# A later norm, a solve in equal portions and ScalarE copies in the chunked scan of a hybrid encoder

## The chip, the cores and the metric

The program runs on one core of a Trainium2 chip. A core has a matrix engine (TensorE, PE in the profile), a vector engine (VectorE, DVE), a scalar engine (ScalarE, ACT), a general engine (GpSimd, POOL) and a queue processor that here only issues transfers (SyncE, SP). Each engine executes its own instructions strictly in order; they wait for each other by semaphores. The metric is the device time of one execution in microseconds, the median of several runs.

## The reference

Two token sequences (256 and 1024 tokens, 1024 channels, 16 heads of 64) go through two layers with the same weights. Layer 0 mixes tokens with a bidirectional RWKV-7 scan, layer 1 with neighbourhood attention, and each is followed by a squared-ReLU MLP. The part that matters here is the scan, run once forward and once backward per head, and the norm behind it:

```python
def step(S, inp):
    r_t, w_t, k_t, v_t, a_t, b_t = inp
    sa = jnp.einsum('bhvk,bhk->bhv', S, a_t)
    S = S * w_t[:, :, None, :] + sa[..., None] * b_t[:, :, None, :] + v_t[..., None] * k_t[:, :, None, :]
    return S, jnp.einsum('bhvk,bhk->bhv', S, r_t)
...
mu = jnp.mean(y, axis=-1, keepdims=True)
var = jnp.mean(jnp.square(y - mu), axis=-1, keepdims=True)
y = ((y - mu) * lax.rsqrt(var + GN_EPS)).reshape(B, T, C) * lnx_g + lnx_b
y = y + (bonus * vf).reshape(B, T, C)
out = (y.astype(h.dtype) * g) @ w_o
```

Here `y` is the sum of both directions, `g` a gate per token and channel, `bonus` a number per token and head.

## The kernel before

The kernel has these stages: dense projections of layer 0 (`l0_proj`), a preparation of the scan's operands that shares the engines with the last projections, the scan (`scan`), then layer 0's output projection and MLP (`channel_layer`), attention, and layer 1's. All dense products are in fp32, split in a high and a low part.

**The scan** works on chunks of 64 tokens. A *job* is 16 chunks of a pair of heads; there are ten jobs, and each step of a job takes one chunk forward and one backward. The written order of the scan is a list of pairs (time, piece of work): `at(t, f)` enters `f` at time `16 j + t` for job `j`, and the list is sorted by time (`scan_until`). That order is kept on PE, DVE, ACT and POOL; SP's order is chosen by the framework. One unit of this time is called a *slot* here: step `i` of a job stands at `16 j + i`. A time outside 0 to 16 falls into the slots of a neighbouring job, so that the stages of several jobs are interleaved:

- *Early products* (L817 to L844; from `T0` = -41 on, eight groups two slots apart): SP loads `eab`, PE multiplies into `aps`, DVE multiplies by a triangular mask into `za` (L837), SP stores `za` to `dd` in DRAM (L840).
- *Rows for the solve* (`mload`, L848, at `T1 = T0 + 17.8`): SP reads `dd` back in another layout into `mt` and `mraw` (L859), POOL copies one half of `mt` transposed (`mtr`, L864, four copies), and clears `q`.
- *The solve* (`rank1`, L870): 31 rows of a triangular system of 32 x 32 blocks, each row two DVE operations, `tmp` (L880) and `q` (L882), and single ones at both ends (L876). From `T2 = T0 + 20.8` on the rows are handed out by an accumulated cost, mostly two rows at one time, 0.67 slots apart, until `T3` = -10.2. `mt`, `mraw` and `q` have one buffer each.
- *Results of the solve* (`qst` L888, `qld` L905): POOL transposes `q` into `qt` (L894), SP stores both to `qd` and loads them back into `Q` and `qx` (tiles `qq`, `qx`; L911, L912).
- *Merges* (L921 to L943; from -5 on): PE multiplies `za` by `qx` into `yps`, ACT copies; PE multiplies into `qps`, ACT copies into `Q`. All these PE results, `aps` and `zps` too, share two PSUM banks.
- *Chunk products* (L955 to L980): four slots ahead of its step, PE computes a chunk pair's products in `kps` (one buffer), ACT copies one part (`ll`, L973), DVE masks the other (`zz`, L968).
- *The step* (`scan_step`): PE, ACT copy `up` (L1043), PE, ACT copy `u` (L1062), PE, two ACT operations for the state `S` (L1077), and the output `y` (L1082, L1085); in the second half of a job DVE adds both directions (L1089).
- *The norm* (`scan_post`): a job's outputs are normed in two halves. Half 0 starts at `t0` = 12.9 of the job, half 1 at 20.9 (in the last job 16.9). Its pieces: `p0` bonus times `vv` on DVE (+0.2), `lnx(1)` the bias added to `bv` on POOL (+0.7), `p1` mean and `p2` centring on DVE (+0.6, +0.95), `p2b` square on ACT (+1.45), `p2c` sum on DVE, `p3` the inverse root on DVE and ACT, `p4` scaling on DVE (+2.5), `lnx(0)` the gain on POOL (L1128, +3.1), `tr` 16 transposing matmuls that add `bv` (`zps`, L1169, +5.4), `p5` a copy on ACT (`zt`, L1173, +5.7) and eight transfers that POOL issues (`z_d`, L1178).

The first jobs' early work is different. Job 0's stands in the preparation's own list (`begin`, L463, maps its times onto that list), and job 1's and a little of job 2's stand in a ramp ahead of the first step. Behind the scan, `gated` multiplies each normed tile by the gate, `t = t * ps` (L1323), and splits it for the output projection.

Of the kernel before, what the change touches and what calls it, by code (L numbers as in the profile page):

```python
# [13 lines left out]
P = 128  # L14
# [15 lines left out]
V_QG, V_KG = 136, 137  # L30
NVEC = 138
# [18 lines left out]
class Trunk:  # L50
# [50 lines left out]
    def l0_proj(self):  # L101
# [361 lines left out]
        def begin():  # L463
            bctx.close()
            self.scan_begin()

            hi, c = -6.0, ((-42.0, tb), (-19.0, tb + 6.0), (-6.0, tb + 17.0))
            for x in self.todo:
                if x[3] < 3 and x[0] <= hi:
                    (x0, t0), (x1, t1) = c[:2] if x[0] < -19.0 else c[1:]  # L470
# [279 lines left out]
    def scan(self):  # L750
# [11 lines left out]
        self.lnx = rp.tile([P, 2, 8, 64], F32, name="lnx")  # L762
        nc.sync.dma_start(self.lnx.rearrange("p a m v -> p (a m v)"), self.a["lnx"])
# [36 lines left out]
    def scan_job(self, j):  # L800
# [8 lines left out]
        b4 = lambda t, n: t.unsqueeze(1).to_broadcast([P, 4, n])  # L809
# [5 lines left out]
        T0 = (-39.0, -39.0, -41.0)[j] if j < 3 else -41.0  # L815
# [4 lines left out]
        for n, (d, g) in enumerate(order):  # L820
# [7 lines left out]
            def prod(h, d=d, g=g):  # L828
# [6 lines left out]
                else:  # L835
                    J["za", d, g] = self.nxt(self.r_za)
                    nc.vector.tensor_tensor(out=J["za", d, g], in0=J["pa"], in1=b4(self.mask[d][:, 0:64], 64), op=ALU.mult)  # L837
# [30 lines left out]
        T3, load, pace = T2, 0.0, (-10.2 - T2) / 15  # L868
        for jj in range(31, 0, -1):
# [129 lines left out]
    def scan_step(self, at, J, st, grp, k, i, new, end):  # L999
# [59 lines left out]
        def s2c():  # L1059
            A, Y, sn, U = banks()  # L1060
            R["u"] = self.sp.tile([P, 2, 64], F32, name="u", tag="u", bufs=2)
# [11 lines left out]
        def s3c():  # L1073
            A, Y, sn, U = banks()
            S = st["S"] = self.sp.tile([P, 2, 64], F32, name="S", tag="S", bufs=3)
# [27 lines left out]
    def scan_post(self, at, J, grp, left):  # L1103

        nc = self.nc
        for half in range(2):
# [16 lines left out]
            def lnx(k, st=st, runs=runs, y=y):  # L1123
                t = (y(), st["bv"].rearrange("p (x c) v -> p x c v", x=2))[k]
                for x in range(1 if runs[0][0] == runs[1][0] else 2):
                    sl = slice(0, 2) if runs[0][0] == runs[1][0] else slice(x, x + 1)
                    w = self.lnx[:, k, runs[x][0]].unsqueeze(1).unsqueeze(1).to_broadcast([P, sl.stop - sl.start, 4, 64])
                    nc.gpsimd.tensor_tensor(out=t[:, sl], in0=t[:, sl], in1=w, op=(ALU.mult, ALU.add)[k])  # L1128
# [42 lines left out]
            def p5(st=st, runs=runs):  # L1171
                zt = self.yp.tile([P, 4, 2, 64], F32, name="zt", tag="ysq", bufs=1)
# [6 lines left out]
            t0 = (12.9, 20.9 if left else 16.9)[half]  # L1179
            if left == 0 and half == 1:  # L1180
                when = (-2.0, -1.9, -0.1, 0.0, 0.1, 0.2, 0.3, 0.4, 0.5, 0.6, 0.65, 0.7, 0.9)
            else:
                when = (0.2, 0.7, 0.6, 0.95, 1.45, 1.75, 1.9, 2.05, 2.25, 2.5, 3.1, *((5.4, 5.7) if left else (4.36, 4.62)))
            for dt, f in zip(when, (p0, lambda f=lnx: f(1), p1, p2, p2b, p2c, lambda f=p3: f(0), lambda f=p3: f(1), lambda f=p3: f(2), p4,
                                    lambda f=lnx: f(0), tr, p5)):
# [122 lines left out]
    def gated(self, wk, pm, src):  # L1308

        nc, act = self.nc, self.act  # L1310
        with self.gctx, self.tc.tile_pool(name="go", bufs=1, reuse_waits="tile", side="right") as gp:
            (sh, sl, ss), (gh, gl, gs) = self.gate
            todo = [(0, k) for k in range(KT)] + [(s, k) for s in (1, 2) for k in range(KT - 1)] + [(1, KT - 1), (2, KT - 1)]
            for s, k in todo:
# [8 lines left out]
                nc.vector.tensor_tensor(out=t, in0=t, in1=ps[:, :n], op=ALU.mult)  # L1323
# [576 lines left out]
def host_layout(inputs):  # L1900
# [25 lines left out]
        np.tile(i["na_q_g"][0], 2)[:, None], np.tile(i["na_k_g"][0], 2)[:, None]], 1)  # L1926
    o["lnx"] = np.stack([np.repeat(i[nm].reshape(8, 2, 64)[:, ::o].transpose(1, 0, 2), 64, 0) for nm, o in (("rw_lnx_g", 1), ("rw_lnx_b", -1))], 1).reshape(P, 1024)
# [36 lines left out]
```

## Time and profile before

| | |
|---|---|
| median of 3 runs | 4191.82 us |
| lowest, highest | 4188.74, 4197.66 us |
| the profiled execution | 4200.27 us |
| its span, from the first to the last instruction | 4198.5 us |
| PE busy | 3843.4 us, 92% |
| DVE busy | 2497.5 us, 59% |
| ACT busy | 1519.9 us, 36% |
| POOL busy | 1294.8 us, 31% |
| first copy `up` of the scan, last one | 770.5 us, 1437.2 us |
| jobs in the scan | 10, of 16 steps |

In a line of a group, "out<-in" are the tiles written and read, then the shapes, "x" and a count; behind the first bar stand the busy microseconds and the mean nanoseconds of one, behind the second the idle time of that engine just before, and what ended it. A line of waits reads: engine, tile and line that waited, what it waited for, microseconds in total, times, the longest. A line of a timeline has start, duration, engine (an engine's name with q is its queue processor, which issues transfers), line, operation, tiles, and in brackets the idle time before it. A line of stretches has its limits and length, then for PE, PE's weight loads, DVE, ACT and POOL the busy time with the number of instructions, the granted share of PE's clock, the mean busy share of the transfer engines, and GB/s.

### The profile page before, as it was taken

The numbers are of one execution on the slowest core, as the hardware profiler recorded it, in microseconds if no ns is written. First come the engines' busy times: TensorE is split into PE (matmuls) and PEld (weight loads), VectorE is DVE, ScalarE is ACT, GpSimd is POOL, SyncE is SP. The second block draws the span as 40 slices with busy tenths as digits, with TensorE's granted clock in tenths as the row PEclk, the third lists the DMA queues.
The fourth block names the chain that finished last, engine by engine and source line by source line (L and its number), as shares of the span: only waits on it lengthen the run. The fifth ranks groups of instructions, "written<-read, shape, count | busy, mean of one in ns | idle before, by whom it ended". The sixth has DMA issues, their size and how long they took to land.

```text
span 4198.5 us, 87027 instructions
## 1 busy us (share of the span) xinstructions
PE 3843.4 (92%) x35188; PEld 3264.8 (78%) x35188; DVE 2497.5 (59%) x4851; ACT 1519.9 (36%) x3651; POOL 1294.8 (31%) x1234
## 2 busy tenths in 40 slices
PE   7887879787888799999999999989988999999999
PEld 4665669687778687888888889867767888888888
DVE  7888973566666457555555562366665755555555
ACT  6776651343444442111111132455554311111111
POOL 5440001133333434222222241244344422222222
PEclk9997889798989899999999999999999999999999
DMA  3326555766564351111111115333334111111111
GB/s 113 87 98 205 195 194 144 199 162 167 152 171 127 88 162 51 36 41 41 36 36 41 41 51 162 96 78 70 81 91 147 61 36 36 41 41 41 36 36 61
DMA packets 385794, 393.48 MB, mean 94 GB/s; under 512 B 161872, under 2 KB 306480, under 8 KB 384112
## 3 DMA queue, kind: packets, MB, share of 16 engines
q1 hardware_dynamic: 331760, 315.42, 26.5%
q10 hardware_dynamic: 46704, 61.35, 4.2%
q0 software_dynamic: 6928, 11.15, 0.9%
q8 instruction: 276, 4.52, 0.4%
q14 instruction: 126, 1.03, 0.1%
HBM read 277.80 MB, written 121.24 MB: 95 GB/s over the span
## 4 chain that ended last, share of the span: by engine, by line
PE 62%; DVE 8%; issue 3%; DMA 3%; POOL 3%; ACT 2%; SPq 1%; ACTq 0%; DVEq 0%; POOLq 0%
PE ps L96 17%; PE ps L98 17%; PE ps L97 17%; PE bx L1001 2%; PE by L1001 1%; DVE q L882 1%; PE kps L963 1%; DVE tmp L880 1%; PE op L1879 1%; PE pt L1821 1%; DVE zz L968 1%; POOL z_d L1178 1%; PE vps L512 1%; PE vps L513 1%; PE vps L514 1%
## 5 line engine op out<-in xcount | busy, mean ns | idle before, releaser
L1436 DVE TENSOR_TENSOR x<-ps,x 128x256 f32<-128x256 f32 x1488 | 813.9, 594 | 629.7 <-PE ps L98 629.3
L96 PE MATMUL ps<-ah,whi 128*128 128x512 f32 (+1 forms) x2304 | 844.7, 367 | 4.9 <-ACT whi L90 4.2
L98 PE MATMUL ps<-ah,wlo 128*128 128x512 f32 (+1 forms) x2304 | 824.8, 358 | 1.8 <-POOL wlo L91 1.8
L97 PE MATMUL ps<-al,whi 128*128 128x512 f32 (+1 forms) x2304 | 824.4, 358 | 0.0
L91 POOL TENSOR_TENSOR wlo<-raw,whi 128x1024 fp32r<-128x1024 f32 (+1 forms) x178 | 390.2, 2192 | 860.9 <-ACT whi L90 833.4
L96 PE MATMUL ps<-hh,whi 128*128 128x512 f32 (+1 forms) x1536 | 548.3, 357 | 11.6 <-DVE x L1436 11.6
L98 PE MATMUL ps<-hh,wlo 128*128 128x512 f32 (+1 forms) x1536 | 547.0, 356 | 0.0
L97 PE MATMUL ps<-hl,whi 128*128 128x512 f32 (+1 forms) x1536 | 546.5, 356 | 0.0
L96 PEld LDWEIGHTS ps<-ah,whi 128*128 128x128 f32 x2304 | 439.7, 191 | 79.6 <-issue 13.2
L98 PEld LDWEIGHTS ps<-ah,wlo 128*128 128x128 f32 x2304 | 438.8, 190 | 67.8 <-POOL wlo L91 2.5
L97 PEld LDWEIGHTS ps<-al,whi 128*128 128x128 f32 x2304 | 439.7, 191 | 60.0 <-issue 1.1
L90 ACT CAST whi<-raw 128x1024 fp32r<-128x1024 f32 (+1 forms) x206 | 200.7, 974 | 703.8 <-PE ps L97 631.5
L96 PEld LDWEIGHTS ps<-hh,whi 128*128 128x128 f32 x1536 | 292.4, 190 | 55.0 <-DVE x L1436 14.0
L1415 POOL TENSOR_TENSOR rl<-rl 128x512 f32<-128x512 f32 (+1 forms) x192 | 174.3, 908 | 500.2 <-PE ps L98 458.3
L98 PEld LDWEIGHTS ps<-hh,wlo 128*128 128x128 f32 x1536 | 292.3, 190 | 41.4
L97 PEld LDWEIGHTS ps<-hl,whi 128*128 128x128 f32 x1536 | 292.3, 190 | 41.3
L1414 ACT ACTIVATE rl<-ps 128x512 f32<-128x512 f32 (+1 forms) x192 | 100.8, 525 | 546.0 <-PE ps L98 546.0
L1417 ACT CAST hh<-rl 128x512 fp32r<-128x512 f32 (+1 forms) x192 | 105.5, 549 | 320.9 <-POOL rl L1415 320.9
L968 DVE TENSOR_TENSOR zz<-kps,cst 128x512 f32<-128x512 f32 x160 | 110.0, 688 | 178.5 <-ACT ll L973 178.3
L1418 DVE TENSOR_TENSOR hl<-rl,hh 128x512 fp32r<-128x512 f32 (+1 forms) x192 | 119.3, 621 | 151.6 <-ACT hh L1417 151.1
L963 PE MATMUL kps<-x 64*64 64x128 f32 (+1 forms) x2560 | 167.6, 327 | 43.1 <-DVE zz L968 40.2
L1814 POOL TENSOR_TENSOR s<-s,mx 128x384 f32<-128x384 f32 (+1 forms) x154 | 116.8, 769 | 213.0 <-DVE mx L1813 149.6
(314 smaller groups left out, 7958.4 us busy)
## 6 DMA issues: line engine op xcount, KB each, us to landing
x<-x_d SPq DMA_DIRECT2D x88, 512.0 KB, 4.6
raw<-in_w_down_dram SPq DMA_DIRECT2D x64, 512.0 KB, 3.5
raw<-in_w_up_dram SPq DMA_DIRECT2D x64, 512.0 KB, 3.5
eab<-x_d SPq DMA_DIRECT2D x80, 256.0 KB, 3.3
x_d<-ar ACTq DMA_DIRECT2D x32, 512.0 KB, 3.1
x_d<-bk ACTq DMA_DIRECT2D x32, 512.0 KB, 4.3
bs<-tab SPq DMA_DIRECT2D x128, 96.0 KB, 3.9
v_d<-vt ACTq DMA_DIRECT2D x80, 128.0 KB, 4.1
```

What stands on the lines that cost most here:

```text
L90: nc.scalar.copy(hi[:, cs], raw)
L91: lo_eng.tensor_tensor(out=lo[:, cs], in0=raw, in1=hi[:, cs].bitcast(F32), op=ALU.subtract)
L96: mm(ps, sh, mh, start=first, stop=False)
L97: mm(ps, sh, ml, start=False, stop=False)
L98: mm(ps, sl, mh, start=False, stop=last)
L963: mm(J["kp"][out, e, 192 * c + 192 - w:192 * c + 192], x[es, b, 2 * pr + c], x[es, 5 - w // 64:5, 2 * pr + c], start=True, stop=True)
L968: nc.vector.tensor_tensor(out=z, in0=src[:, :, :, :P], in1=self.mask[d].unsqueeze(1).unsqueeze(1).to_broadcast([P, 2, 2, P]), op=ALU.mult)
L1001: mm = lambda out, a, b, start, stop: nc.tensor.matmul(out, a, b, start=start, stop=stop, skip_group_check=True)
L1415: nc.gpsimd.tensor_tensor(out=r[:, :n], in0=r[:, :n], in1=r[:, :n], op=ALU.mult)
L1418: nc.vector.tensor_tensor(out=hl[:, :n], in0=r[:, :n], in1=hh[:, :n].bitcast(F32), op=ALU.subtract)
L1436: nc.vector.tensor_tensor(out=xv, in0=ps[:, :n], in1=xv, op=ALU.add)
L1814: nc.gpsimd.tensor_tensor(out=s[:, :nk], in0=s[:, :nk], in1=mx[:, 2:3].to_broadcast([P, nk]), op=ALU.mult)
```

## The change

- *Early products.* `T0` is -41 for jobs 0 and 1 and -43 for the others (before: -39, -39, then -41), so they and the rows for the solve come two slots earlier. ACT copies the product to `za` without the mask. The second half of the product and the copy stand at other fractions of a slot.
- *Solve.* It starts at a time of its own, -21.73 (jobs 0 and 1: -20), in 12 portions of nearly equal written cost, 1.0 slot apart (jobs 0 and 1: 0.8); `T3` is -9.7.
- *Norm.* Half 0 starts at 20.9 and half 1 at 24.9 for all jobs but the last two, which have 12.9 and 16.9.
- *Bias.* POOL no longer adds it to `bv`. It comes with the vectors (`vecs`, eight more columns) and is added in the gate, by a scalar_tensor_tensor in place of the product; the table `lnx` holds the gain alone.
- *Buffers.* `up` and `u` have one buffer instead of two, `S` two instead of three; `zt` no longer shares a buffer with the squares `ysq`.
- *Job 0's early work* is mapped onto the preparation's list with other corner points.

```diff
-            hi, c = -6.0, ((-42.0, tb), (-19.0, tb + 6.0), (-6.0, tb + 17.0))
+            hi, c = -6.0, ((-46.0, tb), (-22.0, tb + 6.0), (-6.0, tb + 17.0))
...
-        T0 = (-39.0, -39.0, -41.0)[j] if j < 3 else -41.0
+        T0 = (-41.0, -41.0)[j] if j < 2 else -43.0
...
-                    nc.vector.tensor_tensor(out=J["za", d, g], in0=J["pa"], in1=b4(self.mask[d][:, 0:64], 64), op=ALU.mult)
+                    nc.scalar.copy(J["za", d, g], J["pa"])
...
-            for h, dt in enumerate((1.74, 2.74, 3.05)):
+            for h, dt in enumerate((1.74, 2.4, 2.62) if j else (1.74, 1.76, 2.04)):
                 at(t + dt, lambda h=h, f=prod: f(h), E)
-            at(t + 3.3, store, E)
+            at(t + 2.9, store, E)
...
         T2 = T1 + 3.0
-        T3, load, pace = T2, 0.0, (-10.2 - T2) / 15
+        T2, T3, pace = (-21.73, -9.7, 1.0) if j > 1 else (-20.0, -9.7, 0.8)
+        cost = [0.0] + [400.0 + 2 * jj * (32 - jj) for jj in range(1, 32)]
...
-            at(T3, rank1, E)
-            load += 400 + 2 * jj * (32 - jj)
-            if load > 930.0:
-                T3, load = T3 + pace, 0.0
+            at(T2 + pace * int(12 * sum(cost[jj + 1:]) / sum(cost)), rank1, E)
...
-            R["up"] = self.sp.tile([P, 2, 64], F32, name="up", tag="up", bufs=2)
+            R["up"] = self.sp.tile([P, 2, 64], F32, name="up", tag="up", bufs=1)
...
-                zt = self.yp.tile([P, 4, 2, 64], F32, name="zt", tag="ysq", bufs=1)
+                zt = self.yp.tile([P, 4, 2, 64], F32, name="zt", tag="zt", bufs=1)
...
-            t0 = (12.9, 20.9 if left else 16.9)[half]
+            t0 = ((20.9, 24.9) if left > 1 else (12.9, 16.9))[half]
...
-                nc.vector.tensor_tensor(out=t, in0=t, in1=ps[:, :n], op=ALU.mult)
+                nc.vector.scalar_tensor_tensor(out=t, in0=t, scalar=self.v(V_LNB, k), in1=ps[:, :n], op0=ALU.add, op1=ALU.mult)
```

More of the change, by code (lines that the diff above doesn't have):

```diff
@@ L1178, in p5 @@
                             nc.gpsimd.dma_start(dst[e, :, c0 + par:c0 + 4:2], zt[64 * par:64 * par + 64, 2 * x:2 * x + 2, e])
[L1179 removed]
+            t0 = ((20.9, 24.9) if left > 1 else (12.9, 16.9))[half]
             if left == 0 and half == 1:
[L1181 removed]
+                when = (-2.0, -0.1, 0.0, 0.1, 0.2, 0.3, 0.4, 0.5, 0.6, 0.65, 0.7, 0.9)
             else:
[L1183 to L1185 removed]
+                when = (0.2, 0.6, 0.95, 1.45, 1.75, 1.9, 2.05, 2.25, 2.5, 3.1, *((5.4, 5.7) if left else (4.36, 4.62)))
+            for dt, f in zip(when, (p0, p1, p2, p2b, p2c, lambda f=p3: f(0), lambda f=p3: f(1), lambda f=p3: f(2), p4, lnx, tr, p5)):
                 at(t0 + dt, f)
```

28 lines of the change are left out of this document (14 added, 14 removed).

## The prediction

> **What bounds the kernel now.** I read the page first, then the busy time by stretch, and then stayed in the scan (about 770 to 1437 us): everything else is dense matmul work that the change hardly touches. A "slot" below is 1.0 of the written time in the scan, one scan step; a job is 16 slots.
>
> ```profile
> span 4198.5 us, 87027 instructions
> PEclk9997889798989899999999999999999999999999
> ```
>
> The span is 4198.5 us. The granted clock dips only in the slices up to the end of the scan. The next view is the busy time in stretches; I cut it at the copies of `up` that open jobs, so that the rows are: the ramp before the first step, job 0, jobs 1 to 7, job 8, and two undisturbed slots of job 4.
>
> ```profile
> core 0: us, PE busy (x) PEld busy (x) DVE busy (x) ACT busy (x) POOL busy (x), PEclk, DMA share, GB/s
> 728.00:770.50 42.50, 21.17 (x380) 19.24 (x378) 12.43 (x34) 4.51 (x12) 12.36 (x33) 0.60 0.85 235
> 770.50:829.40 58.90, 50.21 (x1568) 48.30 (x1568) 40.03 (x105) 26.17 (x107) 6.71 (x12) 0.94 0.70 186
> 829.40:1324.20 494.80, 401.42 (x11863) 387.62 (x11859) 314.32 (x780) 207.52 (x821) 156.21 (x224) 0.91 0.59 158
> 1324.20:1383.00 58.80, 53.43 (x1593) 49.60 (x1592) 36.48 (x84) 29.97 (x120) 19.66 (x26) 0.97 0.44 124
> 1075.30:1081.30 6.00, 6.00 (x220) 6.00 (x218) 1.91 (x4) 3.44 (x15) 1.30 (x3) 1.00 0.46 79
> ```
>
> Jobs 1 to 7 take 494.8 us, 70.7 each, with TensorE busy 401.4. In the two undisturbed slots TensorE is busy all the time at clock 1.00. So a slot has a floor, and TensorE sets it. The timeline of ScalarE (the copy `up` opens each step) gives its length, and the chain gives the extra matmuls of a slot that transposes outputs:
>
> ```profile
> 1078.47 0.27 ACT L1043 COPY up<-bx 128x128 f32<-128x128 f32 x1
> 1081.46 0.27 ACT L1043 COPY up<-bx 128x128 f32<-128x128 f32 x1
> ...
> 1090.16 0.27 ACT L1043 COPY up<-bx 128x128 f32<-128x128 f32 x1
> 1100.33 0.27 ACT L1043 COPY up<-bx 128x128 f32<-128x128 f32 x1 [0.38 <-ACT ll L973]
> 1052.63 2.02 PE zps L1169 x16
> ```
>
> The floor is 1081.46 - 1078.47 = 2.99 us; the step opened at 1090.16 took 10.17. At the floor, seven jobs would need 112 x 2.99 + 14 x 2.02 = 363 us of TensorE. Its 401.4 busy us hold 38 more, spent at a lower clock (0.91 against 1.00), and 494.8 - 401.4 = 93.4 us it is idle. What it waits for, in the same stretch, from the view of waits:
>
> ```profile
> PE kps L963 <- DVE zz L968: 28.1, 13, 4.7
> PE bx L1001 <- ACT u L1062: 16.6, 11, 2.6
> PE zps L1169 <- DVE za L837: 14.7, 12, 2.6
> PE by L1001 <- ACT up L1043: 2.6, 4, 1.0
> ```
>
> VectorE makes TensorE wait 28.1 + 14.7 = 42.8 us, ScalarE 19.2; the other 31.4 are instruction issue, transfers and small pieces. The waits of the two engines themselves say that ScalarE only passes VectorE's lateness on: its `ysq` waits 18.0 us for the norm's `y`.
>
> ```profile
> DVE q L876 <- POOL mt L864: 44.6, 6, 8.5
> ACT ysq L1140 <- DVE y L1136: 18.0, 11, 2.9
> ACT S L1077 <- PE bx L1001: 74.3, 89, 3.5
> ```
>
> And VectorE's own long wait is the solve's first operation, for `mt`. One such stretch, from the timelines of SP, POOL, DVE and PE:
>
> ```profile
> 1071.71 0.34 SPq L896 DMA_DIRECT2D qd<-qt  x1
> 1080.78 0.43 SPq L840 DMA_DIRECT2D dd<-za  x1
> 1084.02 0.78 SPq L859 DMA_DIRECT2D mraw<-dd  x2
> 1087.30 1.01 SPq L912 DMA_DIRECT2D qq<-qd  x2
> ...
> 1089.61 1.61 POOL L864 COPY mt<-mraw 64x256 f32<-64x256 f32 x3 [12.94 <-issue]
> 1091.07 4.78 POOL L1178 DMA_DIRECT2D z_d<-zt  x8
> 1095.78 0.69 POOL L864 COPY mt<-mraw 64x256 f32<-64x256 f32 x1
> 1096.50 0.28 DVE L876 SCALAR_TENSOR_TENSOR q<-mt,q 128x31 f32<-128x31 f32 x1 [8.46 <-POOL mt L864]
> 1097.95 0.59 PE L963 MATMUL kps<-x 64*64 64x192 f32 x4 [4.14 <-DVE zz L968]
> ```
>
> The last product of the next solve reaches SP behind loads of the solve before it (1080.78), so `mraw` goes out at 1084.02 and POOL gets it at 1089.61. Then POOL issues eight output transfers, 4.78 us, between the third and the fourth `mt` copy. VectorE stands at the solve's first operation, the mask `zz` stands behind that, and TensorE waits 4.14 us for `zz`.
>
> **The change, part by part.** Seven jobs first.
>
> *The norm's place.* The same operations are issued, later: half 0 from slot 12.9 to 20.9, half 1 from 20.9 to 24.9 (the last two jobs apart). In slots of the job being scanned, their VectorE work moves from 13.1-16.0 and 5.1-8.0 to 5.1-8.0 and 9.1-12.0. The solve occupied 11.8 to 21.8, so all of half 0's norm lay in its first portions and half 1's in its last; now portions run from 10.27 to 5.27 of the next job and meet only the end of half 1. The eight `z_d` issues of POOL move from slots 2.6 and 10.6 to 10.6 and 14.6, the `mt` copies from 10.3-10.6 to 8.3-8.6, so that no `z_d` is queued ahead of one. The bonus product that frees `vv` moves from 5.1 to 9.1: SP's load of the next `vv` waits for it, and whatever SP has behind it (see the rivals).
>
> *The early products* start two slots earlier. The last store of `dd` moves from 8.3 to 5.9, the load of `mraw` from 8.8 to 6.8, both ahead of the `qq` loads (from 7.3 on before, 7.8 now). In the quoted stretch `mraw` to POOL's first copy took 5.6 us, the copies need some 2; from 6.8 to the solve at 10.27 there are 3.5 slots, 10.4 us at the floor. So the wait for `mt` should go, with 2 to 3 us to spare. What is late next is the solve itself.
>
> *Twelve portions, one per slot.* From the groups of VectorE and ScalarE in the seven jobs:
>
> ```profile
> L882 DVE TENSOR_TENSOR q<-q,tmp 128x247 f32<-128x247 f32 (+14 forms) x203 | 89.9, 443 | 7.0
> L968 DVE TENSOR_TENSOR zz<-kps,cst 128x512 f32<-128x512 f32 x112 | 77.0, 687 | 114.7 <-ACT ll L973 114.6
> L880 DVE TENSOR_TENSOR tmp<-mt,q 128x247 f32<-128x247 f32 (+14 forms) x203 | 72.7, 358 | 4.1
> L837 DVE TENSOR_TENSOR za<-aps,cst 128x256 f32<-128x256 f32 x53 | 21.9, 413 | 0.0
> L1089 DVE TENSOR_TENSOR y<-y,y 128x128 f32<-128x128 f32 x55 | 15.5, 282 | 0.5 <-ACT y L1085 0.5
> L1161 DVE TENSOR_TENSOR y<-y,rqr 128x512 f32<-128x512 f32 x14 | 9.6, 687 | 0.2
> ...
> L973 ACT COPY ll<-kps 128x256 f32<-128x256 f32 x113 | 42.1, 373 | 66.2 <-PE kps L963 53.5 <-DVE q L882 2.8 <-PE bx L1001 2.4
> ```
>
> A solve is (89.9 + 72.7) / 7 = 23.2 us, in portions of 1.9 on average, 2.6 where three rows fall together. A slot asks of VectorE 0.69 (`zz`) + 0.28 (`y`, in half the slots) + 1.9 = 2.9, just under the floor of 2.99. A three-row portion is 0.6 over it; the slot after has two rows and gives it back, and `zz` may be about 1 us late before TensorE's next products need its bank. In slots 10 and 11 the end of half 1 adds some 2 us, but slot 10 is 2.02 longer by the transposes. I leave 8 us of waits on VectorE for seven jobs, a good 1 us per job; between 0 and the present 42.8 it is nearest the floor, because the load is below it.
>
> *Products copied by ScalarE.* VectorE loses 8 x 0.413 = 3.3 us per job. ScalarE gains 8 copies; the nearest row is `ll`, same shape, 0.373: 3.0 us. They stand ahead of the `S` copies, where ScalarE waits for TensorE (74.3 us over 89 times, 0.83 each), so they cost nothing; if that cover were gone, up to 3.0 per job. The bank of the products is then freed without VectorE, and the 14.7 us before `zps` go.
>
> *The bias* leaves POOL (one pass per half) and enters the gate. With it goes a stretch of VectorE that the timelines of POOL and DVE show:
>
> ```profile
> 1101.45 1.26 POOL L1128 TENSOR_TENSOR bv<-bv,lnx 128x512 f32<-128x512 f32 x1 [4.98 <-DVE bv L1121]
> 1101.52 1.35 DVE L882 TENSOR_TENSOR q<-q,tmp 128x135 f32<-128x135 f32 x1
> ```
>
> An operation of about 0.3 us lasted 1.35 beside POOL's pass: 1 us per half. In the gate 24 multiplications get a second operator:
>
> ```profile
> L1323 DVE TENSOR_TENSOR ot<-ot,ps 128x512 f32<-128x512 f32 (+1 forms) x24 | 13.6, 593 | 25.5 <-PE ps L1322 14.1 <-DMA ot<-z_d 11.4
> ```
>
> If it is free they cost 0, if it counts as a second pass 13.6; VectorE is idle 25.5 us ahead of them, so I take 0. Fewer buffers for `up`, `u` and `S`: each is rewritten a slot after its last reader, nothing. `zt` gets a buffer of its own: nothing.
>
> *Ramp.* Job 1's and job 2's products move two slots ahead of the first step, so one more group falls into the stretch 728 to 770.5, where transfers take 0.85 of their engines: 11 or so groups in 42.5 us, +3 us (0 to 6). Job 0's solve ends about one unit of the earlier stage later, ahead of a stretch in which TensorE is half idle: 0.
>
> **The sum.** Waits on VectorE 42.8 - 8 = 35; on ScalarE 19.2 - 3 = 16, as its cause goes; the lost clock 38 - 10 = 28, since it comes back in proportion to the idle time; issue and transfers stay. Jobs 1 to 7: 494.8 - 79 = 416, or 59.4 each. Job 0 (58.9 us, 8.7 of it idle) -4, job 8 (58.8) -2, ramp +3. In all -82 on a profiled execution of 4200.27, span and 1.8 around it: 4118. That execution is 8.5 above the median 4191.82, so I forecast 4110.
>
> On the clock: after the 4.14 us wait above the products ran slower, and the stretch as a whole had 0.91. The Trainium skill (TensorE: Matmul & The Clock Gate, What's actually happening) puts the step to half speed at an idle window of about 3.4 us. By that rule only waits like the 4.14 would cost clock, and with them gone all 38 us come back: 4100, an estimate. The trace has it only in part, since waits of 1 to 2.6 us are most of the idle time and no row ties the clock to one of them.
>
> **The rivals.**
> *The solve still waits for its rows* (faster, less). For: the solve waited for `mt` in six of seven jobs, and SP is in order. Against: the store and the load now precede the `qq` loads. If half of the 79 us stays, 40 come off the gain: about 4150.
> *VectorE becomes the bound of the slot.* For: 2.9 of 2.99. If a portion's slot costs 0.5 more, 12 x 0.5 x 8 = 48 us come off the gain, less the 8 allowed: 4150.
> *The clock stays at 0.91* though the waits go: 28 less, 4138. For: short pieces of issue remain.
> *SP delays the `qq` loads: slower.* Before, from `qd<-qt` to the last `qq` issue SP took 1087.30 - 1071.71 = 15.6 us. From `qst` at 6.3 to the first use of `Q` at 12.1 there are 5.8 slots, 17.4 us at the floor and 2.02 for transposes. If SP stands at `vv` for the bonus product, now four slots later, the loads shift by up to 12 us, and TensorE stands for about 12 + 5.6 (landing) + 15.6 + 2 - 19.4 = 16 us in each job, more than the 11.3 that a job gains: 7 x 4.7 = 33, so about 4225. It decides from a shift of about 8 us. Against: one slot of lateness is the most I see in the written order.
> *Nothing:* each wait is replaced by an equal one, 4192.
>
> **How the numbers follow.** Forecast 0.60, rows late 0.10, VectorE 0.10, clock 0.08: all faster, 0.88. Nothing 0.04. SP 0.08, slower. Within 0.2% (8 us), which is about what a measurement here can tell, is the same. The low end: no residue on VectorE or ScalarE and all the clock, 21 more, and half of the 31.4 of issue and transfers, as they come where transfers crowd: 4110 - 37 = 4073. The high end takes in the three weaker gains with 10 us over: 4160. About 0.15 is left out.
>
> **What would show it.** Right: the solve's first operation without a wait for `mt`; no wait of `zps` for `za`; steps of 3.0 us in most slots and 5.0 in slots 10 and 14; `ysq` without a wait; the clock above 0.95 in jobs 1 to 7; VectorE at about 39 us a job. Wrong: waits of TensorE for `qq` or `qx`; SP standing at `vv`; `zz` waits of 1 us and more in slots 12 to 15; a longer ramp.

## The result and the profile after

The changed kernel takes 4157.59 us (median of 4 runs, 4147.27 to 4166.45), the kernel before 4190.83 in the same session. The ratio is 0.9917, with a 95% interval of 0.9891 to 0.9943: a gain of about 33 us, where 82 were forecast. The profiled execution of the changed kernel took 4156.58 us against 4200.27 before, 43.7 less. From the copies `up`, the first of the scan stands at 773.6 us (before 770.5) and the last at 1387.0 (before 1437.2), so the scan from first to last step is 53.3 us shorter; behind it the program is 6.3 us longer. There the second MLP, whose code the change does not touch, takes 866.4 us against 859.1, from the end of its last `nps` matmul to the end of the program. The other traces divide in the same way: 858.7 to 859.2 us in the versions of the kernel before, 864.6 to 866.9 in those of the changed kernel. So the 7 us come with the change, and why they do stays open.

Page of the changed kernel, the span and the granted clock:

```profile
span 4154.6 us, 86991 instructions
...
PEclk9997889899999899999999999999999999999999
```

Busy time by stretch of the changed kernel, cut at the same copies as before: the ramp, job 0, jobs 1 to 7, job 8. Behind the solve, line numbers are three or four lower than before.

```profile
731.10:773.60 42.50, 19.98 (x342) 18.30 (x338) 12.04 (x33) 8.04 (x21) 10.17 (x27) 0.56 0.89 213
773.60:834.00 60.40, 48.13 (x1568) 45.75 (x1568) 32.72 (x85) 28.30 (x112) 6.80 (x11) 0.97 0.75 200
834.00:1279.30 445.30, 390.57 (x11840) 370.83 (x11840) 295.71 (x728) 225.93 (x873) 132.37 (x205) 0.96 0.68 174
1279.30:1336.10 56.80, 53.16 (x1592) 49.59 (x1592) 35.36 (x83) 30.60 (x122) 16.02 (x24) 0.97 0.49 128
```

Jobs 1 to 7 went from 494.8 to 445.3 us. TensorE's idle time there fell from 93.4 to 54.7 us and its busy time from 401.4 to 390.6; the clock rose from 0.91 to 0.96, and the transfer engines' share from 0.59 to 0.68, the same transfers in less time. What TensorE waits for in this stretch:

```profile
PE by L998 <- issue: 10.8, 10, 2.4
PE qps L934 <- issue: 10.2, 6, 3.2
PE bx L998 <- issue: 9.4, 8, 2.1
PE kps L960 <- issue: 7.0, 6, 2.1
PE bx L998 <- ACT u L1059: 6.3, 6, 1.4
PE aps L833 <- issue: 5.4, 4, 2.0
PE by L998 <- ACT up L1040: 3.1, 9, 0.4
PE yps L922 <- issue: 2.2, 3, 1.1
```

No wait for VectorE is left; before they came to 43.8 us. VectorE's own list has no `mt` any more, only its normal rhythm:

```profile
DVE zz L965 <- ACT ll L970: 137.0, 92, 4.8
DVE va L1141 <- ACT ysq L1137: 0.2, 1, 0.2
```

So the change did to VectorE what it was forecast to do. But the waits that the profile calls *issue*, in which TensorE waits for no other engine and no data, grew from 25.3 us to 45.0.

**What these waits are.** One of them in the timeline of TensorE (start, duration, operation; in brackets the idle time before):

```profile
1031.75 0.61 PE L934 MATMUL qps<-qq,yt 64*64 64x32 f32 x16
1032.19 0.25 PE L998 MATMUL by<-up,qq 64*64 64x64 f32 x1
1034.83 0.39 PE L998 MATMUL by<-up,qq 64*64 64x64 f32 x6 [2.39 <-issue]
```

TensorE stops between the first and the second of eight equal matmuls, with the operands there. Counting its instructions over the trace (matmuls, weight loads and its semaphore instructions together), all 37 of these waits in jobs 1 to 7 fall at multiples of 256 instructions from one starting point, to within two. The view of transfers of jobs 1 to 7 has the counterpart:

```profile
q8 instruction: 93, 1.52, 1.4%
```

93 packets, 1.52 MB, so 16,384 bytes each, for 11840 matmuls and 11840 weight loads: one packet for 255 of them, with the semaphore instructions 256. TensorE's code is fetched while the program runs, through the same transfer engines as the data, 256 instructions (a *block*) at a time, and TensorE stops when the next block has not come. The view of transfers from 1032.1 to 1033.4 us, in which the packet ahead of this gap's end was moved:

```profile
q1 hardware_dynamic: 455, 0.44, 102.5%
q8 instruction: 1, 0.02, 5.4%
```

All 16 engines were full of data (0.99 in the 3.6 us before the gap as well, in the stretches quoted further down); the code packet began at 1032.19 and ended at 1033.31, 1.5 us before TensorE went on. The block before the gap had begun at 1028.53, so the packet started 3.7 us after that; where transfers are few (the run with light loads below) the median is 1.1 us. In jobs 1 to 7, 35 of the 93 packets started more than 2 us after the beginning of their block, packets and blocks paired in order, and the gaps at the blocks behind them make up 42 of the 45 us.

The end of the packet also sets the end of the gap. At the 32 code gaps of over 0.3 us in jobs 1 to 7, TensorE went on 1.2 to 1.8 us after the end of the packet that had started in the block before; at the 53 of the run with heavy loads below it was 1.2 to 1.7 us. By an estimate from these figures, a block of 3.6 us leaves a packet of 1.1 us, followed by 1.4 us, a start at most 1.1 us after the block begins: the usual start is just in time, and any delay costs TensorE.

The Trainium skill (DMA: Bandwidth & Descriptors, Queues, rings and completion order) says that a transfer engine takes its queues in turn, a packet of typically 9 to 17 descriptors at a time. By that rule, with 55 ns for a piece of 1024 bytes (40,694 of them took 2228 us here), a code packet would be held up 0.5 to 0.9 us, an estimate; the trace has starts up to 4.4 us behind a block's beginning, 3.3 more than the usual 1.1.

### The profile page after: what moved, and what is told of

The parts are those of the page before. It is cut to its first block, busy times and chain, and to the rows that moved or that the text cites. A ratio compares the mean times of both kernels' runs of the same rounds, so it can differ in the third digit from the quotient of the medians.

```text
span 4154.6 us, 86991 instructions
## 1 busy us (share of the span) xinstructions
PE 3837.0 (92%) x35188; PEld 3233.9 (78%) x35188; DVE 2459.8 (59%) x4771; ACT 1547.9 (37%) x3731; POOL 1262.3 (30%) x1210
## 3 DMA queue, kind: packets, MB, share of 16 engines
q14 instruction: 126, 1.03, 0.1%
## 4 chain that ended last, share of the span: by engine, by line
PE 72%; DVE 13%; issue 4%; ACT 4%; DMA 4%; POOL 2%; SPq 1%; ACTq 0%; DVEq 0%; POOLq 0%
PE ps L96 17%; PE ps L97 17%; PE ps L98 17%; PE by L998 3%; PE bx L998 3%; PE kps L960 2%; PE vps L512 1%; PE vps L513 1%; PE vps L514 1%; PE zps L1166 1%; PE op L1875 1%; DVE cs L628 1%; PE pt L1817 1%; PE aps L833 1%; PE yps L922 1%
## 5 line engine op out<-in xcount | busy, mean ns | idle before, releaser
L91 POOL TENSOR_TENSOR wlo<-raw,whi 128x1024 fp32r<-128x1024 f32 (+1 forms) x178 | 390.6, 2195 | 864.3 <-ACT whi L90 836.8
L97 PEld LDWEIGHTS ps<-al,whi 128*128 128x128 f32 x2304 | 437.2, 190 | 65.4 <-issue 1.1
L97 PEld LDWEIGHTS ps<-hl,whi 128*128 128x128 f32 x1536 | 291.4, 190 | 40.9
```

The costliest lines, as they stand in the source:

```text
L91: lo_eng.tensor_tensor(out=lo[:, cs], in0=raw, in1=hi[:, cs].bitcast(F32), op=ALU.subtract)
L97: mm(ps, sh, ml, start=False, stop=False)
```

## The experiments

Theory A: the data loads delay TensorE's code, so every wait that goes brings the next fetch forward and turns in part into a wait for code. Rival B: code is late because TensorE uses it faster than it can be fetched, whatever else is moved. Rival C: VectorE's load still sets the slot. All times of jobs 1 to 7 below are from one profiled execution of each kernel, cut at `up` of slot 0 of jobs 1 and 8.

### Fewer bytes, the same instructions

The buffers are also cleared once, ahead of the scan (not shown in the cut).

```diff
-                nc.sync.dma_start(J["e", d, g], self.x_d[m, d, 0:4:2, :, tok(c0)].rearrange("x p (c t) -> p x c t", c=4))
+                nc.sync.dma_start(J["e", d, g][:, :, 0:1], self.x_d[m, d, 0:4:2, :, c0 * L:c0 * L + L].rearrange("x p (c t) -> p x c t", c=1))
...
-                nc.sync.dma_start(J["x", d, g][:, 0:4], self.x_d[m, d, :, :, tok(c0)].rearrange("x p (c t) -> p x c t", c=4))
+                nc.sync.dma_start(J["x", d, g][:, 0:4, 0:1], self.x_d[m, d, :, :, c0 * L:c0 * L + L].rearrange("x p (c t) -> p x c t", c=1))
```

> The changed kernel, but the loads of the scan's operands (`eab` for the early products, `x4` for the chunk products) fetch one chunk of each four; the same instructions on all engines, the output is not the reference's. In jobs 1 to 7 this takes 1024-byte pieces that hold 2228 of 4844 us of transfer-engine time down to 256 bytes (55 ns to about 21 ns each), so the transfer engines' share falls from 0.68 to about 0.49. Theory A (TensorE's instruction code, 16,384 bytes for 256 instructions, arrives late because data transfers stand before it): issue waits of TensorE in jobs 1 to 7 fall from 45 to under 25 us, the clock rises from 0.96 to 0.98 or more, jobs 1 to 7 from 445 to 405 to 425 us. Rival B (code is late because TensorE uses it faster than it can be fetched, whatever else is moved): issue waits stay at 45 +- 5, jobs 1 to 7 at 445 +- 5. Rival C (VectorE's load sets the slot): also 445 +- 5.

One run, 4081.04 us, beside 4194.86 for the kernel before. Its stretch and its first waits:

```profile
810.50:1205.50 395.00, 375.61 (x11840) 357.31 (x11840) 296.34 (x729) 226.57 (x873) 132.58 (x205) 0.99 0.52 117
```

```profile
PE bx L1001 <- ACT u L1062: 9.9, 7, 1.7
PE by L1001 <- ACT up L1043: 3.2, 9, 0.4
PE bx L1001 <- issue: 3.1, 6, 1.0
```

Jobs 1 to 7 lost another 50 us, more than theory A gave it, with the issue waits at 5.8 us in all and the clock at 0.99. TensorE, VectorE and ScalarE execute the same work as before the cut. Rivals B and C are out. Packets that start more than 2 us late: 5 of 93.

### More bytes

```diff
+        self.dram("junk", [2, 4, P, 256])
...
                 nc.sync.dma_start(J["x", d, g][:, 0:4], self.x_d[m, d, :, :, tok(c0)].rearrange("x p (c t) -> p x c t", c=4))
+                nc.sync.dma_start(self.scr["junk"][n % 2], self.x_d[m, d, :, :, tok(c0)])
```

> The changed kernel with one more transfer behind each `x4` load, a copy of the same operands from DRAM to DRAM that nothing reads: some 28,700 more pieces of 1024 bytes in jobs 1 to 7, 55 ns each, 1570 us of transfer-engine time on 4844; share 0.68 to about 0.88. Theory A: issue waits in jobs 1 to 7 rise from 45 to 70 or more, jobs 1 to 7 from 445 to 475 or more, the clock falls below 0.95. Rival B and rival C: 445 +- 8, issue waits 45 +- 8, apart from waits that are named for data.

One run, 4241.11 us. The stretch and the first waits:

```profile
843.20:1355.90 512.70, 410.32 (x11840) 389.65 (x11840) 292.92 (x728) 226.13 (x872) 132.70 (x205) 0.91 0.76 203
```

```profile
PE by L1000 <- issue: 28.5, 15, 4.2
PE bx L1000 <- issue: 19.4, 11, 3.0
PE kps L962 <- issue: 17.1, 9, 3.5
```

67 us more, issue waits of 97.6 us, the clock back at 0.91, and 56 of 93 packets late. The transfers' share is 0.76, not the 0.88 expected, as the stretch grew. Theory A holds in both directions: data that nothing waits for slows TensorE through its code.

### What the change is worth without the crowd

The same cut of the loads in the kernel before; the diff is that of the first experiment.

> The kernel before with the loads of `eab` and `x4` cut to one chunk of four, as in the changed kernel with light loads (the output is not the reference's). Jobs 1 to 7 took 494.8 us before and 445.3 changed; with light loads the changed kernel took 395.0. Theory A (the change took VectorE's waits away as forecast, and the code fetch gave half of it back): here the issue waits fall from 25 to under 8 us, the VectorE waits of TensorE stay at 43 +- 8, and jobs 1 to 7 take 460 to 475, so that with light loads the change is worth 65 to 80 us, near the 79 forecast. Rival (the waits of before come from late transfers too, so that light loads take them away as well): VectorE waits under 25, jobs 1 to 7 under 445, and the change worth 50 us or less in both.

One run, 4187.42 us. The stretch and the first waits:

```profile
825.70:1311.40 485.70, 396.20 (x11861) 384.40 (x11858) 314.76 (x781) 207.98 (x822) 156.45 (x224) 0.92 0.43 96
```

```profile
PE kps L966 <- DVE zz L971: 37.9, 14, 5.7
PE bx L1004 <- ACT u L1065: 22.7, 13, 3.4
PE zps L1172 <- DVE za L840: 15.4, 12, 2.6
```

The kernel before gains only 9 us from lighter loads, less than expected: issue waits fall to 8.4 us, but VectorE's waits grow from 43.8 to 53.3 and ScalarE's from 19.6 to 25.1. With light loads the change is worth 485.7 - 395.0 = 91 us in jobs 1 to 7, more than expected; with full loads 49.5. So the 79 us of the prediction were there to be had, and late code took a good part of them back. The two kernels stood under different limits: VectorE before, code after.

### The parts, one at a time

The norm's old times in the changed kernel:

```diff
-            t0 = ((20.9, 24.9) if left > 1 else (12.9, 16.9))[half]
+            t0 = (12.9, 20.9 if left else 16.9)[half]
```

> The changed kernel with the norm's old starting times (12.9 and 20.9). The prediction's working (the norm's VectorE work and the output transfers on POOL collide with the solve): VectorE waits of TensorE come back in jobs 1 to 7, 15 to 30 us of them, the clock falls to 0.93 or 0.94, jobs 1 to 7 take 470 to 490 us; 4180 to 4200 in all. Rival (the norm's place is worth little since the code fetch fills the gaps that it leaves): jobs 1 to 7 445 to 455, within 10 us of 4158.

4167.56 us (4 runs), ratio to the kernel before 0.9936 (0.9918 to 0.9953). Jobs 1 to 7 took 452.4 us, 7 more than the changed kernel, with no wait for VectorE: the rival's side. (Its profiled execution was the slowest of the four, 8 us above the median, so the 7 us are a rough figure.)

The copy to `za` by VectorE again:

```diff
-                    nc.scalar.copy(J["za", d, g], J["pa"])
+                    nc.vector.tensor_tensor(out=J["za", d, g], in0=J["pa"], in1=self.mask[d][:, 0:64].unsqueeze(1).to_broadcast([P, 4, 64]), op=ALU.mult)
```

> The changed kernel with the early products copied by VectorE again (with the mask). The prediction's working: 8 x 0.41 us of VectorE per job come back on a slot that VectorE fills to 2.9 of 2.99, and the copy is queued behind solve portions; 15 us of waits on `za` and `zz` in jobs 1 to 7, with their clock: jobs 1 to 7 460 to 470 us, 4172 to 4182 in all. Rival (the code fetch sets the pace, VectorE has room): 445 +- 5 and within 6 us of 4158.

4146.89 us, ratio 0.9889 (0.9867 to 0.9912), jobs 1 to 7 448.4. The total lies 11 below the changed kernel's, more than the 6 that were allowed for, but the intervals overlap and jobs 1 to 7 are 3 us longer. VectorE was busy 310.7 us in place of 295.7, and TensorE waited 1.1 us for it.

The old portions of the solve:

```diff
-        T2, T3, pace = (-21.73, -9.7, 1.0) if j > 1 else (-20.0, -9.7, 0.8)
+        T3, load, pace = T2, 0.0, (-10.2 - T2) / 15
...
-            at(T2 + pace * int(12 * sum(cost[jj + 1:]) / sum(cost)), rank1, E)
+            at(T3, rank1, E)
+            load += 400 + 2 * jj * (32 - jj)
+            if load > 930.0:
+                T3, load = T3 + pace, 0.0
```

> The changed kernel with the solve's rows handed out by the old accumulated cost between the old kind of limits (from T1 + 3.0 to -10.2), all else as changed. The prediction's working (portions of 2.6 us on VectorE against a slot of 2.99): VectorE waits of 5 to 15 us come back, jobs 1 to 7 452 to 465. Rival (the code fetch sets the pace, and VectorE has room for an uneven slot): jobs 1 to 7 445 +- 6, within 8 us of 4158.

4155.00 us, ratio 0.9905 (0.9886 to 0.9924), jobs 1 to 7 445.2: no difference. None of the three parts, taken back alone, brings more than 1.1 us of waits for VectorE: it has room for any of them, and the code sets the pace.

Then two parts alone in the kernel before. The norm's new times (the line above, the other way round):

> The kernel before with the new starting times of the norm (20.9 and 24.9) and nothing else. The prediction's working (the output transfers that POOL issues ahead of the last `mt` copy, and the norm in the solve's first portions, make VectorE late): the wait of the solve's first operation for `mt` falls from 44.6 to under 25 us, jobs 1 to 7 from 494.8 to 465 to 480, 4165 to 4180 in all. Rival (the rows are late by their own start, on SP, and the norm's place does not matter): jobs 1 to 7 495 +- 8, 4185 to 4200.

4152.89 us, ratio 0.9912 (0.9883 to 0.9941): the whole gain of the change, from one line. Jobs 1 to 7 took 459.4, less than expected and 14 more than in the changed kernel; but its first step comes 10 us earlier (763.5 against 773.6), and its second MLP takes 859.2 us in place of 866.4. But VectorE still waits for the rows:

```profile
DVE q L876 <- POOL mt L864: 40.4, 7, 7.4
```

That is 40.4 us against 44.6, and POOL's timeline shows why, here for one job:

```profile
1123.22 1.67 POOL L864 COPY mt<-mraw 64x256 f32<-64x256 f32 x3 [7.34 <-DMA mraw<-dd]
1124.74 4.79 POOL L1178 DMA_DIRECT2D z_d<-zt  x8
1129.47 0.68 POOL L864 COPY mt<-mraw 64x256 f32<-64x256 f32 x1
```

With the new times the output transfers of half 0 take the place that those of half 1 had (20.9 + 5.7 is slot 10.6 in both), so in all seven jobs POOL still issues eight of them ahead of the last `mt` copy. The run therefore does not test that cause. What fell are TensorE's waits for `za` (14.7 to 6.1 us) and for ScalarE (19.6 to 3.7), those for `zz` only a little (28.1 to 24.4), and the time that the clock lost (granted clock 0.91 to 0.95). The wait of `ysq` for the norm's `y` fell too, from 18.0 to 5.7, which fits the other half of the prediction's cause, the norm on the solve's first portions.

The early products and rows two slots earlier, and nothing else:

```diff
-        T0 = (-39.0, -39.0, -41.0)[j] if j < 3 else -41.0
+        T0 = (-41.0, -41.0)[j] if j < 2 else -43.0
...
-            hi, c = -6.0, ((-42.0, tb), (-19.0, tb + 6.0), (-6.0, tb + 17.0))
+            hi, c = -6.0, ((-46.0, tb), (-22.0, tb + 6.0), (-6.0, tb + 17.0))
...
-                    (x0, t0), (x1, t1) = c[:2] if x[0] < -19.0 else c[1:]
+                    (x0, t0), (x1, t1) = c[:2] if x[0] < -22.0 else c[1:]
```

> The kernel before with the early products, and so the rows for the solve, two slots earlier (T0 at -41 and -43, and the corner points of job 0 with it); norm, copies, portions and bias as before. The prediction's working (the solve waited for `mt` because the rows were loaded too late): VectorE's wait for `mt` falls from 44.6 to under 12 us, TensorE's waits for `zz` and `za` from 43 to under 20, jobs 1 to 7 from 494.8 to 450 to 468; so each of the two remedies, the norm's place (459.4 alone) and the early rows, would do most of the gain alone. Rival (the norm that still falls on the solve's first portions keeps VectorE late): jobs 1 to 7 475 to 495.

4167.16 us, ratio 0.9929 (0.9908 to 0.9950), jobs 1 to 7 467.4. Here the wait for the rows goes:

```profile
DVE q L876 <- POOL mt L864: 11.3, 5, 3.8
```

The waits for `zz` fall from 28.1 to 2.5 us, those for `za` rise to 20.9 (23.4 together, where under 20 were expected), and issue waits to 40.9. Two things changed for `mt` here: the rows start earlier, and the four copies now stand together ahead of the output transfers, in all seven jobs. The runs don't separate the two. Eight issues of 4.8 us in each of seven jobs are 33 us, so the transfers may well be the larger part of the 40.4, an estimate.

The two remedies overlap: 35 us in jobs 1 to 7 from the one, 27 from the other, 49.5 for the whole change. To see whether the norm's place is worth little beside early rows, or whether late code hides it, its old times were tried again with light loads:

> The changed kernel with the loads of `eab` and `x4` cut to one chunk of four (the output is not the reference's) and with the norm's old starting times. With full loads the old times cost 7 us in jobs 1 to 7 (452.4 against 445.3). Theory A (full loads hide what a part of the change is worth, since a wait taken away lets the code fetch come due instead): with light loads the old times cost more, 15 to 35 us on 395.0: jobs 1 to 7 410 to 430, with waits for `zz`, `u` and `up` grown. Rival (with the early rows in place the norm's time hardly matters): 395 to 405.

One run, 4114.25 us.

```profile
817.10:1234.50 417.40, 377.32 (x11840) 359.94 (x11840) 294.81 (x730) 227.02 (x872) 135.06 (x208) 0.98 0.50 111
```

```profile
PE bx L1001 <- ACT u L1062: 21.8, 14, 2.0
PE by L1001 <- ACT up L1043: 7.1, 15, 0.8
```

The old times cost 22 us with light loads and 7 with full ones. With light loads they bring waits for ScalarE back, for `u` and `up` (28.9 us against 13.1). With full loads these grow less (14.7 against 9.4): a part of what the norm's place is worth is hidden behind waits for code.

### Moving the same bytes apart

```diff
-                nc.sync.dma_start(J["x", d, g][:, 0:4], self.x_d[m, d, :, :, tok(c0)].rearrange("x p (c t) -> p x c t", c=4))
-            at(2 * n - 10.0, kload)
+                (nc.gpsimd if j else nc.sync).dma_start(J["x", d, g][:, 0:4], self.x_d[m, d, :, :, tok(c0)].rearrange("x p (c t) -> p x c t", c=4))
+            at(2 * n - (9.0 if j else 10.0), kload)
```

> The changed kernel with the `x4` loads of all jobs but the first issued by POOL, whose order is the written one, at 2 n - 9 instead of by SP at 2 n - 10: SP issued each right beside an `eab` load and up to six loads within 3 us (from 1027.28 to 1030.31). The same bytes. Theory A1 (a code packet waits behind a bunch of loads, so their placing counts): issue waits in jobs 1 to 7 fall from 45 to 20 to 35 us, jobs 1 to 7 to 420 to 437, 4130 to 4150 in all. Rival A2 (only the mean load of the transfer engines counts): issue waits 45 +- 6, jobs 1 to 7 440 to 452.

4160.85 us, ratio 0.9920 (0.9898 to 0.9941). Jobs 1 to 7 took 437.0 with 38.8 us of issue waits, 8 and 6 less than the changed kernel, but job 0 took 65.4 (60.4), and the total did not move. The issue waits lie between the two expectations, and 30 packets are late in place of 35: most of the lateness stays when bunches are pulled apart. The Trainium skill (DMA: Bandwidth & Descriptors, Issuing engines are not separate DMA queues) has it that all issuing engines feed the same 16 transfer engines. The unchanged total does not speak against that, but shows no more.

### Fewer bytes, all of the work

Two of the four arrays that the late load fetches have been in `eab` 35 slots earlier. With 17 buffers in place of 4 they can stay:

```diff
+        ek = self.ectx.enter_context(tc.tile_pool(name="ek", bufs=1, reuse_waits="tile", side="right"))
+        self.r_e[0] += [ek.tile([P, 2, 4, 64], F32, name=f"eab{4 + i}") for i in range(13)]
...
-                J["x", d, g] = self.nxt(self.r_x4)
-                nc.sync.dma_start(J["x", d, g][:, 0:4], self.x_d[m, d, :, :, tok(c0)].rearrange("x p (c t) -> p x c t", c=4))
+                x = slice(1, 4, 2) if 0 < j < 9 else slice(0, 4)
+                nc.sync.dma_start(J["x", d, g][:, x], self.x_d[m, d, x, :, tok(c0)].rearrange("x p (c t) -> p x c t", c=4))
+            def keep(d=d, g=g):
+                J["x", d, g] = self.nxt(self.r_x4)
+                if 0 < j < 9:
+                    nc.scalar.copy(J["x", d, g][:, 0:4:2], J["e", d, g])
+            at(2 * n - 11.45, keep)
```

> The changed kernel with fewer bytes to move: in jobs 1 to 8 the two arrays of `eab` stay in 17 buffers (4 before) until ScalarE copies them into `x4`, and the late load fetches the other two arrays alone. In jobs 1 to 7 a third of the 1024-byte pieces goes, 743 of 4844 us of transfer-engine time. Theory A, by proportion between the changed kernel and the runs with light and heavy loads (-1390 us gave -50 us, +1433 gave +67): jobs 1 to 7 from 445 to 409 to 422, issue waits from 45 to 18 to 30 us, 4118 to 4138 in all. Rival (56 copies of some 0.6 us on ScalarE, 34 us, delay `up` and `u` and eat the gain): jobs 1 to 7 435 to 450.

4125.26 us (5 runs, 4122.5 to 4131.98), ratio to the kernel before 0.9833 (0.9818 to 0.9847): 70 us faster than before, and below the changed kernel's 4157.59. The stretch and the first waits:

```profile
815.80:1240.70 424.90, 383.56 (x11840) 361.46 (x11840) 299.02 (x728) 251.61 (x928) 132.57 (x205) 0.98 0.60 149
```

```profile
PE kps L968 <- issue: 10.2, 9, 2.0
PE bx L1006 <- ACT u L1067: 7.8, 8, 1.7
PE bx L1006 <- issue: 7.1, 8, 2.1
```

Jobs 1 to 7 came down 20 us, to 3 us above the range expected, and the issue waits to 29.6. ScalarE is busy 25.7 us longer for the 56 copies and makes TensorE wait 11.0 us in all (9.4 before the step), so the copies cost next to nothing. This version beats both kernels.

With its late loads on POOL as well:

> The version that keeps two arrays of `eab`, with its late loads issued by POOL at 2 n - 9 as in the run that only moved them there (which took jobs 1 to 7 from 445.3 to 437.0 and left the total where it was). If bunches of loads still make code late: jobs 1 to 7 from 424.9 to 412 to 420, 4112 to 4122 in all. If the mean load alone counts: 425 +- 6, within 8 us of 4125.

4125.11 us, ratio 0.9837 (0.9814 to 0.9860), jobs 1 to 7 424.3: nothing, as far as the total goes.

The runs side by side, jobs 1 to 7 of one execution each, in microseconds (late: code packets out of 93 that start more than 2 us after the beginning of their block, packets and blocks paired in order):

```
kernel                        jobs 1-7   issue   VectorE  ScalarE  clock  share  late
before                          494.8     25.3     43.8     19.6    0.91   0.59    26
before, light loads             485.7      8.4     53.3     25.1    0.92   0.43     7
before, norm's new times        459.4     32.5     30.5      3.7    0.95   0.65    34
before, early rows              467.4     40.9     23.4     12.2    0.96   0.62    31
changed                         445.3     45.0      0.0      9.4    0.96   0.68    35
changed, norm's old times       452.4     51.6      0.0     14.7    0.97   0.67    44
changed, light loads            395.0      5.8      0.0     13.1    0.99   0.52     5
changed, light, old times       417.4     10.8      0.0     28.9    0.98   0.50    13
changed, heavy loads            512.7     97.6      0.0      4.5    0.91   0.76    56
two arrays kept                 424.9     29.6      0.0     11.0    0.98   0.60    22
```

More late packets go with longer issue waits, run by run, almost without exception. Before, 26 packets were late and the gaps behind them came to 20.5 us; after, 35 and 42.2.

## Why the prediction was wrong

The direction and the place were right. The size was wrong: 82 us forecast, about 33 measured. That 4157.59 still lies in the stated range is luck: its upper part, up to 4160, was there for rows that come late, for VectorE as the bound and for a clock that stays, and none of these came.

Between the two profiled executions the gain is 43.7 us. Of the 38 us that are short of 82, jobs 1 to 7 are 29.5 (49.5 gained where 79 were forecast), job 0 is 5.5, and the stages behind the scan, which the sum left out, 6.3; the last job, left out too, gained 3.3. Between 43.7 and 33 lie 10 us that come from the choice of executions: the profiled one of the kernel before was 8.5 us slower than the median 4191.82.

- **"Issue and transfers stay" is the step that failed.** The sum entered them as 0. Issue waits grew by 45.0 - 25.3 = 19.7 us; the waits for transferred data that were named as such (3.6 us, `qq`) went, so the term is +16. The prediction treated issue as a property of the instruction stream, and at the low end of the range even let half of it go. It is a transfer with a deadline: when the same bytes had to pass in less time, more packets were late (35 against 26).
- **The lost clock** was near, and a term beside it was missing: forecast -28 us of busy time (38 to 10), measured -10.8. Jobs 1 to 7 have 11 stretches at half clock where before had 18, each beside a gap in TensorE, and after the change all of these gaps are for code. With light loads three were left. Half of each such stretch (3.4 us, some before 6.8) is time lost: 42.7 us before, 18.8 after, so the clock gave back 23.9. The rest of the busy time rose from 358.7 to 371.8 us, 13.1 more, and the sum has no term for that.
- **The floor of a slot, taken as unchanged, rose** in every second slot. The changed kernel's copies `up` at the ends of two undisturbed slots, the first with the second half of an early product, the other with the first half:

```profile
1038.82 0.27 ACT L1040 COPY up<-bx 128x128 f32<-128x128 f32 x1 [0.27 <-PE bx L998]
1041.93 0.27 ACT L1040 COPY up<-bx 128x128 f32<-128x128 f32 x1
...
1104.92 0.27 ACT L1040 COPY up<-bx 128x128 f32<-128x128 f32 x1
1107.91 0.27 ACT L1040 COPY up<-bx 128x128 f32<-128x128 f32 x1
```

  They are slots 3 and 4 of a job, 3.11 and 2.99 us, with 109 matmuls each; before, both took 2.99. Slot 1 went from 2.99 to 3.10, slot 7 from 2.79 to 3.02 (medians of the slots with no gap and no half clock). The change moved the second half of the early product from 2.74 to 2.4, between the products that read `zz` and those that read `u`; the first half stayed at 1.74. The versions of the kernel before with the norm's new times or with the early rows have 2.99 in slot 3, all three versions of the changed kernel with one part taken back 3.10 and more. That is some 1 us a job, 7 of the 13 us by an estimate from these slots; the other 6 stay open.
- **VectorE's waits**: forecast -35, measured -43.8, none left against the 8 that I had left. The portions, which I took to be just under the floor, could be uneven again at no cost, and the copies could go back to VectorE at 1.1 us of waits: the slot had more room than 2.9 of 2.99. VectorE was busy 295.7 / 112 = 2.64 us a slot, and a slot lasted 3.98 on average. (A job took 42.2 us of VectorE, where the prediction named 39.)
- **ScalarE's waits**: forecast -16, measured -10.2. `ysq` still waits for the norm's `y`, 7.7 us in place of 18.0.
- **The cause given for `mt`** was not refuted, but not shown part by part either. In the changed kernel the four copies stand together and the wait is gone. Earlier rows alone bring that order and leave 11.3 us; the norm's new times alone leave the transfers between the copies, and 40.4 us. The prediction set the better order down to both moves (no `z_d` ahead of a copy); the earlier rows alone bring it.
- **Small terms**: ramp +3 forecast, and the first step comes 3.1 us later; job 0 -4, but +1.5 came, with transfers at 0.75 of their engines there; job 8 -2, and -2.0 came. The gate's multiplications take 652 ns in place of 593, 1.4 us for 24, and from the start of the first to that of the last 31.0 us in place of 30.4: the 0 was near enough.
- **The rivals**: no wait of TensorE for `qq` or `qx` is left, so SP's order did no harm; VectorE is not the bound; the rows are not late. "The clock stays" named the right cause, short pieces of issue, and the wrong effect: the clock rose to 0.96, while these waits did not remain as they were but grew.

The terms for jobs 1 to 7 add up: -43.8 - 10.2 + 19.7 - 3.6 on idle time, less 0.8 of small pieces, and -23.9 + 13.1 on busy time are -49.5.

## What to carry to other kernels

Where the profile puts waits down to issue, count the instructions between them and look at the packets of kind instruction: if the gaps come at a fixed number of instructions, the engine's code is a load with a deadline, and any data moved beside it competes with it. A forecast that takes waits away must then put the same bytes into the shorter time, and ask how many more fetches come late; here heavier and lighter data at equal instructions gave that slope in two runs, +67 and -50 us in jobs 1 to 7. Bytes that are fetched twice are then worth removing even where no engine waits for them. A change of the written order that is made beside the main one (here 0.34 of a slot for one product) needs a term of its own, too.

## What the runs showed of the hardware

- TensorE's code comes in packets of 16,384 bytes for 256 instructions while the program runs, 276 of them in the whole execution. At the floor of 2.99 us a step, with some 106 matmuls and as many weight loads, 256 instructions last 3.6 us. A packet itself takes 1.1 us on average; it is mostly its start that slips.
- Half clock came after short gaps. The stretches of the changed kernel around the gap quoted above, with the granted clock in the third column from the end:

```profile
1028.50:1032.10 3.60, 3.60 (x134) 3.42 (x128) 2.57 (x6) 2.58 (x11) 0.32 (x1) 1.00 0.99 335
1032.50:1034.80 2.30, 0.00 (x0) 0.00 (x0) 2.13 (x6) 0.00 (x0) 0.00 (x0) 1.00 1.07 345
1034.90:1038.20 3.30, 3.30 (x78) 3.30 (x80) 0.00 (x0) 0.98 (x5) 0.00 (x0) 0.54 0.37 96
1039.00:1041.00 2.00, 2.00 (x86) 2.00 (x86) 1.58 (x5) 1.13 (x6) 0.00 (x0) 1.00 0.30 49
```

After 2.39 us of idling TensorE ran 3.41 us at half clock. In jobs 1 to 7 of the changed kernel each of the 11 such stretches lies beside a gap of 1.66 to 3.17 us, and none of the 14 gaps of 1.03 to 1.58 us has one. The rule that the prediction weighed, the Trainium skill's (TensorE: Matmul & The Clock Gate, What's actually happening) of an idle window of about 3.4 us, has the length of the slow stretch right; the idling that brought it on was shorter here. The limit of 1.6 us is no rule for the other runs: with heavy loads gaps of up to 3.1 us have no such stretch beside them, and with light loads one of 1.54 us has.
